# The last columns of the final product and their norm: two pieces over two pairs of row blocks become three pieces over four

## The chip, the cores and the metric

The kernel runs on one core of a Trainium2 chip. On that core five engines work side by side: TensorE (PE in the profile, PEld for its weight loads), VectorE (DVE), ScalarE (ACT), GpSimd (POOL) and SyncE (SP), which issues the DMA transfers. Each engine executes its own instructions strictly in the order in which the program gives them, and waits where an operand or a buffer is not ready. The metric is the device time of one execution in microseconds.

## The reference, cut to what matters

The reference is one layer of a hybrid decoder on 1024 positions of width 1024, and a norm at its end:

```
h = rmsnorm(x);  p = h @ W_in
x = x + concat(gated delta rule(p), gated linear recurrence(p)) @ W_out
x = x + relu(rmsnorm(x) @ W1)**2 @ W2          # W1: 1024 x 4096, W2: 4096 x 1024
y = x * rsqrt(mean(x*x, axis=-1) + 1e-6) * final_norm_w
```

The change touches the end of the last two lines: a part of the product with W2, the sum of squares over the 1024 channels, its reciprocal square root, and the multiplication of each value by that root and by the channel's weight in `final_norm_w`.

## The kernel before, in words

Data lie with channels on the 128 partitions and positions in the free dimension. A tile is 128 channels by 512 positions (a slab), and the 1024 channels of the result are eight such blocks, here called 0 to 7, for each of two halves of the positions. There are 84 slabs and eight PSUM banks, and both are handed on from use to use.

`layer()` does not issue instructions while it runs. It records each operation with a due time in a plan (class `Plan`, L181). At the end `Plan.emit` (L281) walks through time with its own cost model (`Plan.price`, L260, and for TensorE the cost handed to `pl.unit`), takes for each engine the operation that is ready with the smallest due time, and issues it at L371. So nearly every instruction of the profile stands at L371 and is told apart by the names of its tiles. The order that comes out is fixed in the program; if on the chip something takes longer than the model thinks, the engine waits and does not look for other work.

The product with W2 is done with seven block products in place of eight, in the scheme of Strassen and Winograd: the contraction is cut into 16 groups, the weights of each group into four blocks, and product *i* multiplies a sum of weight blocks v*i* with a sum of activation blocks u*i*. Four stages hold the products (1,7), (6,5), (2,4) and (3). Here only the last stage matters, product 3. For each group *g* DVE computes the block v3 as a difference (written over the loaded slab `w2r`, with the saved sum `s`), ACT rounds it to a high part `v3h` and DVE computes the low part `v3l`; in the same way u3 is loaded as `ur` and split into `u3h` and `u3l`. For each of four output blocks *d* and each group, `mm3` issues three matmuls into one PSUM bank `p`: u3h with v3h, u3l with v3h, u3h with v3l. All have a weight tile of 128 x 128 and a moving tile of up to 512 columns, which are positions.

In stage 3, groups 0 to 13 (NG - 2) run pair by pair over 512 columns into four banks. Behind group 13 DVE adds the four banks to the slabs `u2[d]` (in the profile `u<-p,u`), which hold the other products and the residual `x2` (`u<-x,u`). Then the last two groups, 14 and 15, run in two halves of 256 columns, four banks each, and for each half:

- DVE adds the bank to `u2[d]`, ACT squares the sum (`sq`), and ACT writes it once more multiplied by the norm weight (`xf`);
- `normed` (L1332) sums the squares over channels with matmuls whose weight is a tile of squares and whose moving tile is one column, `onesd` (`n3p`, one per 128 positions and tile of squares);
- ACT takes the square root, DVE the reciprocal and a Newton step (`ms`, `n3r`, `rst`), and a matmul spreads the result over the partitions (`n3b`);
- DVE multiplies `n3b` with each of the eight weighted blocks, four that ACT weighted earlier (`p5`, written over themselves; in the rows `p__9614` and the like) and four of `xf`, into slabs `ot` that hold two blocks of 256 columns each, and SP issues one DMA of 256 KB for each.

The due times of the products come first with half 0, then half 1; the additions and the squares have earlier due times than the products, so each engine takes them as soon as the cost model has them ready. The other three quarters of the result (blocks of positions or channels that are ready earlier) are normed in stage 3 beside the products.

Of the kernel before, what the change touches and what calls it, by code (L numbers as in the profile page):

```python
# [9 lines left out]
AF = mybir.ActivationFunctionType  # L10
ALU = mybir.AluOpType
# [19 lines left out]
DO = [0, 4, 1, 5, 2, 6, 3, 7]  # L31
KEEP_T = 8
LOOK = 4
SLACK = 1.0
LAND = 2.0
EPS = 1e-6
# [349 lines left out]
def layer(ctx: ExitStack, tc: tile.TileContext, xT, win, wba, prm, cst, wga, wgx, wout, w1, w2, out):  # L386
# [3 lines left out]
    pl = Plan()  # L390
    pe, ve, ac, gp, sy = (pl.engine(n) for n in engines)
# [9 lines left out]
    def slab(nm, dt=F32):  # L401
        return pl.tile(sp, [P, 512], dt, "s", nm)
# [4 lines left out]
    def bank(nm):  # L407
        return pl.tile(mpool, [P, 512], F32, "m", nm)
# [29 lines left out]
    PIECE = 0.68  # L438

    def mm3(ps, w, x, first, last, order=((0, 0), (0, 1), (1, 0))):  # L440
        n = 0
        for a, b in order:
            pe.matmul(ps, lhsT=w[a], rhs=x[b], start=first and n == 0, stop=last and n == 2)
            n += 1
# [9 lines left out]
    def par(nm, i=0, n=1):  # L454
        o = PRM[nm][0]
        return pr[:, o + i:o + i + n]
# [17 lines left out]
    with pl.at(due=-5000.0):  # L474
        wz = slab("wz")
        ve.memset(wz, 0.0)
        ps = bank("wz")
# [500 lines left out]
    def chain(t):  # L978
        return pl.at(due=t)
# [9 lines left out]
    with pl.at(due=-2000.0):  # L989
        for hf in range(2):  # L990
# [3 lines left out]
            for k in range(KT):  # L994
                pl.due = -2000.0 + 10 * k + 100 * hf
                if hf == 0:
                    xraw[0, k] = slab("xraw")
                    sy.dma_start(out=xraw[0, k], in_=xT[k * P:(k + 1) * P, hs])
                    if k in (0, 2, 4):
                        n = 4 if k == 4 else 2  # L1000
# [87 lines left out]
    for i in range(2, len(MT)):  # L1088
        mt = MT[i]
        split(i + 1)  # L1090
        for hf in range(2):
            ps = gemm(i if hf == 0 else None, f"pj{mt}", KT, lambda k: (ksl(wt[mt], k), (xh[hf][k], xl[hf][k])), 10000.0 + when(i))
# [41 lines left out]
    for n, d in enumerate(DO):  # L1134
        i = len(MT) + n
        t = when(i)
        split(i + 1)
        for hf in range(2):
            ps = gemm(i if hf == 0 else None, "po", KT, lambda k: (ksl(wt["o", d], EO[k]), M3[EO[k], hf]), 10000.0 + t)
# [5 lines left out]
            with chain(t + 7 + 7 * hf):  # L1145
# [3 lines left out]
                x = bm[d, hf] = slab("bm")  # L1149
# [17 lines left out]
    NG = NF // 2  # L1167
# [37 lines left out]
    for g in range(NG):  # L1205
        t = tf(g)
# [61 lines left out]
    def ts(st, g):  # L1268
        return begin[st] + g * 2.72 * len(STAGES[st])
# [50 lines left out]
    def wsl(g, i, d):  # L1320
        return tuple(t[:, d * P:(d + 1) * P] for t in W2[g, i])
# [9 lines left out]

    def normed(X, parts, a, n, t, lead, end):  # L1332

        m = n // P
        one = bank("n3p") if len(parts) == 1 else None
        pn = [one[:, c:c + 1] if one is not None else bank("n3p")[:, 0:1] for c in range(m)]
        for k, (x, ready) in enumerate(parts):
            with chain(ready):
                with pl.unit(0.12 * m):
                    for c in range(m):  # L1340
                        pe.matmul(pn[c], lhsT=x[:, c * P:(c + 1) * P], rhs=onesd, start=k == 0, stop=k == len(parts) - 1)
        with chain(t):
            r, v = small("n3r", [P, 4])[:, 0:m], small("ms", [P, 4])[:, 0:m]
            if end:
                for c in range(m):
                    ac.activation(out=r[:, c:c + 1], in_=pn[c], func=AF.Sqrt, bias=eps)
                    ve.tensor_scalar_add(out=v[:, c:c + 1], in0=pn[c], scalar1=EPS)
                ve.reciprocal(out=r, in_=r)
                newton(r, v)
            else:  # L1350
                ve.tensor_scalar_add(out=v, in0=one[:, 0:m], scalar1=EPS)
                rsqrt(r, v)
            pb = bank("n3b")
            with pl.unit(0.22 * m):
                rows(pb, r, m)
            g = 512 // n
            for j, d in enumerate(lead):
                if j % g == 0:
                    ot = slab("ot")
                y = ot[:, j % g * n:j % g * n + n]  # L1360
                if not end:
                    ve.scalar_tensor_tensor(out=y, in0=X[d], scalar=par("fnw", d), in1=pb[:, 0:n], op0=ALU.mult, op1=ALU.mult)
                else:
                    ve.tensor_tensor(out=y, in0=pb[:, 0:n], in1=X[d], op=ALU.mult)
                if (j + 1) % g == 0:
                    b = lead[j + 1 - g]
                    sy.dma_start(out=out[b * P:(b + g) * P, a:a + n].rearrange("(d p) t -> p d t", p=P),
                                 in_=ot.rearrange("p (d t) -> p d t", d=g))

    def squares(x, n=512):  # L1370
        y = slab("sq3")[:, 0:n]
        ac.activation(out=y, in_=x, func=AF.Square)
        return y
# [4 lines left out]
        residual[2] += [(x, (d + o, hf), 1 + 4 * n + d) for d in range(4)]  # L1378
    residual[3] = [(u2, (d, 1), 3 + 2 * d) for d in range(4)]
    for st, prods in enumerate(STAGES):  # L1380
        tail = 2 if st == 3 else 0
        pd = {}
        for g0 in range(0, NG, 2):
            gs = (g0, g0 + 1)
            for g in gs:
                get2(st, g)
            if st == 3 and g0 == NG - tail:
                break
            end = g0 == NG - tail - 2
            for d in range(4):  # L1390
                for i in prods:
                    if g0 == 0:
                        pd[i, d] = bank("p2")
                    for g in gs:
                        with pl.at(due=10000.0 + ts(st, g0) + 0.1 * d, keep={"m": 0}), pl.unit(PIECE):
                            mm3(pd[i, d], wsl(g, i, d), UU[g, i], g == 0, end and g == gs[1])
                        if d == 0 and i == prods[-1]:
                            seen[st * NG + g] = pl.ops[-1]
                    if not end:
                        continue  # L1400
                    ps = pd[i, d]
                    with chain(ts(st, g0) - 100):
                        if i in (1, 7, 5):
                            x = {1: p1, 7: u3, 5: p5}[i][d] = slab(f"p{i}_")
                            ac.copy(out=x, in_=ps)
                        elif i == 6:
                            u2[d] = slab("u2")
                            ve.tensor_tensor(out=u2[d], in0=ps, in1=p1[d], op=ALU.add)
                        elif i == 2:
                            plus(p1[d], ps)  # L1410
                        elif i == 4:
                            plus(u3[d], ps)
                        else:
                            plus(u2[d], ps)
            for x, k, g in residual[st]:
                if g in gs:
                    with chain(ts(st, g) + 3):
                        plus(x[k[0] % 4], load_x2(*k, st, g))
                        if x is p5:
                            y = squares(p5[k[0] % 4])  # L1420
                            if k[0] == 4:
                                ss = y
                            else:
                                plus(ss, y)
        t = begin[st] + 87
        if st == 1:

            with chain(t + 5):
                for d in range(4):
                    plus(u3[d], u2[d])  # L1430
                    plus(u2[d], p5[d])
                    plus(p5[d], u3[d])
        if st == 2:
            with chain(t - 40):
                s1 = None
                for x in [p1[d] for d in range(4)] + [u3[d] for d in range(4)]:
                    y = squares(x)
                    if s1 is None:
                        s1 = y
                    else:  # L1440
                        plus(s1, y)
            normed([p1[d] for d in range(4)] + [u3[d] for d in range(4)], [(s1, t - 40)], 0, 512, t - 30, list(range(KT)), False)

    t = ts(3, NG - 2)
    with pl.at(due=-1000.0, gate=seen[3 * NG + 4]):
        ac.activation(out=one("root", [P, 1]), in_=onesd, func=AF.Sqrt, bias=eps)
    with chain(t - 60):
        for d in range(4):
            ac.activation(out=p5[d], in_=p5[d], func=AF.Copy, scale=par("fnw", d + 4))
    for o in (0, 256):  # L1450
        qs = slice(o, o + 256)
        parts = []
        xs = {}
        for d in range(4):
            ps = bank("p2")[:, 0:256]
            for g in range(NG - 2, NG):
                with pl.at(due=10000.0 + t + o / 50 + 0.1 * d), pl.unit(PIECE / 2):
                    mm3(ps, wsl(g, 3, d), tuple(x[:, qs] for x in UU[g, 3]), g == NG - 2, g == NG - 1)
            with chain(t - 100):
                x = u2[d][:, qs]  # L1460
                plus(x, ps)
                parts.append((squares(x, 256), t))
                xs[d] = slab("xf")[:, 0:256]
                ac.activation(out=xs[d], in_=x, func=AF.Copy, scale=par("fnw", d))
        parts.insert(1, (ss[:, qs], t))
        X = [xs[d] for d in range(4)] + [p5[d][:, qs] for d in range(4)]
        normed(X, parts, 512 + o, 256, t + o / 50, [4, 5, 6, 7, 0, 1, 2, 3], True)

    pl.emit(engines, caps)

# [62 lines left out]
```

## Time and profile before

| what | value |
| --- | --- |
| three timed runs | 1111.16, 1112.57, 1112.77 us; median 1112.57 |
| the profiled execution | 1111.17 us, its span 1109.4 us |
| PE busy | 1089.9 us, 98% of the span |
| PEld busy | 898.4 us, 81% |
| DVE busy | 855.8 us, 77% |
| ACT busy | 559.0 us, 50% |
| POOL busy | 101.2 us, 9% |
| share of PE in the chain of work that ended last | 81% |
| DMA | mean 136 GB/s over the span |

The profile is that of one execution. Its durations and starts are in microseconds from the start of the span, and what the chip needs before and after the span is in the execution's own time. [...] Matmuls follow each other in a pipeline, so a row of one matmul is longer than the distance from its start to the next one's start; that distance is what a matmul costs when many stand in a row. A row "x4" is four instructions of one kind in succession. A matmul in full precision, as `n3p` and `n3b` are, appears as two passes, and so as twice as many rows as the program has instructions.

### The profile page before, as it was taken

The page shows a single profiled execution, that of the slowest core. Times are in us where ns is not written, and L with a number is a line of the kernel's source. Part 1 is how long each engine was busy: PE and PEld are TensorE (multiplying, and loading weights), DVE is VectorE, ACT ScalarE, POOL GpSimd, SP SyncE. Part 2 cuts the span into 40 slices and gives each one's busy share as a digit, 9 for nine tenths or more (in the row PEclk, how much of TensorE's full clock was granted, in tenths as well). Part 3 has the DMA queues.
Part 4 walks back from the last instruction along what each step waited for, and adds up shares of the span by engine and source line. Part 5 has one row for each costly group of instructions (what it writes and reads, how often), then busy time and mean ns, then how long its engine had stood idle before and what let it go on. Part 6 is the DMA issues. An engine that isn't in the chain of part 4 may idle for free.

```text
span 1109.4 us, 15927 instructions
## 1 busy us (share of the span) xinstructions
PE 1089.9 (98%) x5439; PEld 898.4 (81%) x5439; DVE 855.8 (77%) x1656; ACT 559.0 (50%) x1144; POOL 101.2 (9%) x282
## 2 busy tenths in 40 slices
PE   8999999999999999999999999999999999999996
PEld 6788877888887778888888888888888888888885
DVE  7868575696779777598988888887965767775786
ACT  8568545453485955453433333333544544464443
POOL 0002654736000000000000000000000000000000
PEclk9999999999999999999999999999999999999997
DMA  6122132031110144433634344434856565576382
GB/s 238 39 77 82 30 101 46 28 91 27 42 39 19 39 138 145 145 104 130 212 142 155 144 166 143 171 138 173 285 179 215 183 204 189 198 244 233 131 293 78
DMA packets 88128, 150.77 MB, mean 136 GB/s; under 512 B 22344, under 2 KB 25072, under 8 KB 88048
## 3 DMA queue, kind: packets, MB, share of 16 engines
q1 hardware_dynamic: 88048, 149.77, 40.2%
q8 instruction: 42, 0.69, 0.3%
q14 instruction: 38, 0.31, 0.1%
HBM read 110.91 MB, written 38.82 MB: 135 GB/s over the span
## 4 chain that ended last, share of the span: by engine, by line
PE 81%; DVE 5%; POOL 5%; ACT 3%; issue 2%; SPq 2%; DMA 1%; DVEq 0%; POOLq 0%; ACTq 0%
PE p L371 28%; PE pf L371 28%; PE pj L371 11%; PE po L371 7%; POOL V L371 2%; POOL tm L371 2%; SPq L371 2%; PE pvs L371 1%; DVE y L371 1%; PE psr L371 1%; PE psO L371 1%; DVE ig L371 1%; PE psba L371 1%; ACT rg L371 1%; PE psZ L371 1%
## 5 line engine op out<-in xcount | busy, mean ns | idle before, releaser
L371 PE MATMUL pj<-xh,w 128*128 128x512 f32 x704 | 246.6, 406 | 0.2 <-DVE U L371 0.2
L371 PEld LDWEIGHTS pj<-xh,w 128*128 128x128 f32 x704 | 132.7, 188 | 27.3 <-DVE U L371 0.4
L371 PE MATMUL pj<-xl,w 128*128 128x512 f32 x352 | 137.7, 391 | 0.0
L371 ACT ACTIVATE c<-c 128x512 f32<-128x512 f32 x64 | 40.4, 632 | 86.3 <-DVE c L371 80.8
L371 ACT CAST w<-r 128x512 fp32r<-128x512 f32 (+1 forms) x62 | 51.3, 829 | 60.6 <-PE pf L371 36.4
L371 PE MATMUL po<-mxh,w 128*128 128x512 f32 x256 | 78.9, 389 | 0.0
L371 PEld LDWEIGHTS pj<-xl,w 128*128 128x128 f32 x352 | 66.8, 190 | 10.1
L371 DVE SCALAR_TENSOR_TENSOR y<-p,pr,y 128x512 f32<-128x512 f32 (+3 forms) x96 | 71.3, 747 | 4.1 <-ACT y L371 3.1
L371 DVE TENSOR_TENSOR w<-r,w 128x512 fp32r<-128x512 f32 (+1 forms) x62 | 58.8, 949 | 18.3 <-ACT w L371 17.9
L371 POOL TENSOR_TENSOR tm<-V,N 128x60 f32<-128x60 f32 (+24 forms) x124 | 46.6, 376 | 133.1 <-DMA N<-bn 91.8
L371 PEld LDWEIGHTS po<-mxh,w 128*128 128x128 f32 x256 | 48.1, 188 | 9.9
L371 PE MATMUL po<-mxl,w 128*128 128x512 f32 x128 | 49.9, 390 | 1.5 <-DVE mxl L371 1.5
L371 POOL TENSOR_TENSOR V<-V,tm 128x60 f32<-128x60 f32 (+24 forms) x124 | 47.8, 385 | 9.7
L371 DVE SCALAR_TENSOR_TENSOR c<-c,n2B 128x512 f32<-128x512 f32 x64 | 43.7, 687 | 1.2
L371 PE MATMUL pf<-B6h,w 128*128 128x512 f32 x128 | 42.5, 391 | 0.0
L371 PE MATMUL pf<-B5h,w 128*128 128x512 f32 x128 | 42.5, 393 | 0.0
L371 ACT ACT_TABLE_LOAD x29 | 37.2, 1283 | 1.2 <-PEq L1526 0.7
L371 DVE TENSOR_TENSOR c<-pf,u 128x512 f32<-128x512 f32 x48 | 32.7, 684 | 0.5
L371 DVE TENSOR_TENSOR p<-pj,n1B 128x512 f32<-128x512 f32 x28 | 19.2, 686 | 17.5 <-PE pj L371 17.4
L371 ACT CAST v6h<-s 128x512 fp32r<-128x512 f32 x16 | 10.0, 623 | 40.2 <-DVE s L371 40.2
L371 PEld LDWEIGHTS po<-mxl,w 128*128 128x128 f32 x128 | 24.0, 188 | 6.9 <-DVE mxl L371 1.9
L371 PEld LDWEIGHTS pf<-B5h,w 128*128 128x128 f32 x128 | 24.0, 188 | 6.8 <-DVE c L371 1.9
(515 smaller groups left out, 2982.2 us busy)
## 6 DMA issues: line engine op xcount, KB each, us to landing
w2r<-w SPq DMA_DIRECT2D x112, 256.0 KB, 3.4
ur<-ud SPq DMA_DIRECT2D x112, 256.0 KB, 4.9
r<-w SPq DMA_DIRECT2D x32, 512.0 KB, 3.7
ud<-c SPq DMA_DIRECT2D x64, 256.0 KB, 2.1
ud<-ut SPq DMA_DIRECT2D x48, 256.0 KB, 2.2
r<-win SPq DMA_DIRECT2D x22, 512.0 KB, 3.7
xraw<-xT SPq DMA_DIRECT2D x16, 256.0 KB, 5.3
r<-wout SPq DMA_DIRECT2D x8, 512.0 KB, 4.2
```

The lines of the kernel that those rows point to most:

```text
L371: getattr(engines[e], method)(*[v.ap() if isinstance(v, View) else v for v in args], **{k: v.ap() if isinstance(v, View) else v for k, v i ...
```

## The change

The last four groups (12 to 15) are now held back in place of the last two, and run in three pieces of 256, 128 and 128 columns in place of two halves. The cost that the plan is told for three matmuls is now a formula in their width. The weighted copies `xf` and the earlier weighting of `p5` go; the last multiply takes the weight as a third operand (`scalar_tensor_tensor`) and gets a due time 20 us later than the rest of its piece. An `ot` slab holds at most two blocks, so that pieces of 128 columns leave in DMAs of 128 KB, whose rows are 128 values long. Everything before group 12 of stage 3 stands on PE and on SP as it stood. In the rows below, `p_...` with a number is a PSUM bank.

```diff
@@ -31,6 +31,7 @@
 DO = [0, 4, 1, 5, 2, 6, 3, 7]
 KEEP_T = 8
 LOOK = 4
+TAIL = 4
 SLACK = 1.0
 LAND = 2.0
 EPS = 1e-6
@@ -1353,19 +1354,17 @@
             pb = bank("n3b")
             with pl.unit(0.22 * m):
                 rows(pb, r, m)
-            g = 512 // n
+            g = min(512 // n, 2)
             for j, d in enumerate(lead):
                 if j % g == 0:
                     ot = slab("ot")
                 y = ot[:, j % g * n:j % g * n + n]
-                if not end:
+                with chain(t + 20):
                     ve.scalar_tensor_tensor(out=y, in0=X[d], scalar=par("fnw", d), in1=pb[:, 0:n], op0=ALU.mult, op1=ALU.mult)
-                else:
-                    ve.tensor_tensor(out=y, in0=pb[:, 0:n], in1=X[d], op=ALU.mult)
                 if (j + 1) % g == 0:
                     b = lead[j + 1 - g]
                     sy.dma_start(out=out[b * P:(b + g) * P, a:a + n].rearrange("(d p) t -> p d t", p=P),
-                                 in_=ot.rearrange("p (d t) -> p d t", d=g))
+                                 in_=ot[:, 0:g * n].rearrange("p (d t) -> p d t", d=g))
 
     def squares(x, n=512):
         y = slab("sq3")[:, 0:n]
@@ -1378,14 +1377,14 @@
         residual[2] += [(x, (d + o, hf), 1 + 4 * n + d) for d in range(4)]
     residual[3] = [(u2, (d, 1), 3 + 2 * d) for d in range(4)]
     for st, prods in enumerate(STAGES):
-        tail = 2 if st == 3 else 0
+        tail = TAIL if st == 3 else 0
         pd = {}
         for g0 in range(0, NG, 2):
             gs = (g0, g0 + 1)
             for g in gs:
                 get2(st, g)
-            if st == 3 and g0 == NG - tail:
-                break
+            if g0 >= NG - tail:
+                continue
             end = g0 == NG - tail - 2
             for d in range(4):
                 for i in prods:
@@ -1441,30 +1440,24 @@
                         plus(s1, y)
             normed([p1[d] for d in range(4)] + [u3[d] for d in range(4)], [(s1, t - 40)], 0, 512, t - 30, list(range(KT)), False)
 
-    t = ts(3, NG - 2)
+    t = ts(3, NG - TAIL)
     with pl.at(due=-1000.0, gate=seen[3 * NG + 4]):
         ac.activation(out=one("root", [P, 1]), in_=onesd, func=AF.Sqrt, bias=eps)
-    with chain(t - 60):
+    for o, n in ((0, 256), (256, 128), (384, 128)):
+        qs = slice(o, o + n)
+        parts = []
         for d in range(4):
-            ac.activation(out=p5[d], in_=p5[d], func=AF.Copy, scale=par("fnw", d + 4))
-    for o in (0, 256):
-        qs = slice(o, o + 256)
-        parts = []
-        xs = {}
-        for d in range(4):
-            ps = bank("p2")[:, 0:256]
-            for g in range(NG - 2, NG):
-                with pl.at(due=10000.0 + t + o / 50 + 0.1 * d), pl.unit(PIECE / 2):
-                    mm3(ps, wsl(g, 3, d), tuple(x[:, qs] for x in UU[g, 3]), g == NG - 2, g == NG - 1)
+            ps = bank("p2")[:, 0:n]
+            for g in range(NG - TAIL, NG):
+                with pl.at(due=10000.0 + t + o / 50 + 0.1 * d), pl.unit(3 * (n + 32) / 2400):
+                    mm3(ps, wsl(g, 3, d), tuple(x[:, qs] for x in UU[g, 3]), g == NG - TAIL, g == NG - 1)
             with chain(t - 100):
                 x = u2[d][:, qs]
                 plus(x, ps)
-                parts.append((squares(x, 256), t))
-                xs[d] = slab("xf")[:, 0:256]
-                ac.activation(out=xs[d], in_=x, func=AF.Copy, scale=par("fnw", d))
+                parts.append((squares(x, n), t))
         parts.insert(1, (ss[:, qs], t))
-        X = [xs[d] for d in range(4)] + [p5[d][:, qs] for d in range(4)]
-        normed(X, parts, 512 + o, 256, t + o / 50, [4, 5, 6, 7, 0, 1, 2, 3], True)
+        X = [u2[d][:, qs] for d in range(4)] + [p5[d][:, qs] for d in range(4)]
+        normed(X, parts, 512 + o, n, t + o / 50, [4, 5, 6, 7, 0, 1, 2, 3], True)
 
     pl.emit(engines, caps)
 
```

Three places show what the plan makes of it. The first is DVE at group 12 of stage 3, before; `s_8529` and `s_8562` are the saved sums of groups 12 and 13, and `v3l` and the first `u3l` behind it belong to group 12.

```order
L371 TENSOR_TENSOR w2r<-w2r,s_8529 128x512
L371 TENSOR_TENSOR u_9664<-x_10768,u_9664 128x512
L371 TENSOR_TENSOR v3l<-w2r,v3h 128x512
L371 TENSOR_TENSOR u3l<-ur,u3h 128x512
L371 TENSOR_TENSOR w2r<-w2r,s_8562 128x512
```

The same place now, where `p_10512`, `p_10527` and `p_10544` are the banks of the products up to group 11.

```order
L372 TENSOR_TENSOR w2r<-w2r,s_8529 128x512
L372 TENSOR_TENSOR u_9664<-x_10764,u_9664 128x512
L372 TENSOR_TENSOR u_9600<-p_10512,u_9600 128x512
L372 TENSOR_TENSOR u_9630<-p_10527,u_9630 128x512
L372 TENSOR_TENSOR v3l<-w2r,v3h 128x512
L372 TENSOR_TENSOR u_9664<-p_10544,u_9664 128x512
L372 TENSOR_TENSOR u3l<-ur,u3h 128x512
L372 TENSOR_TENSOR w2r<-w2r,s_8562 128x512
```

Three additions from PSUM have moved in among the preparations of group 12, two ahead of `v3l` and one more ahead of `u3l`.

The second place is the end of PE's order, before: the last product's last two matmuls, the sums of squares (`n3p`) of the second half and the broadcast of its result.

```order
L371 MATMUL p_10954<-u3l,v3h 128x256
L371 MATMUL p_10954<-u3h,v3l 128x256
L371 MATMUL n3p<-onesd,sq_11009 128x1 x2
L371 MATMUL n3p<-onesd,sq_11019 128x1 x2
L371 MATMUL n3p<-onesd,sq_9848 128x1 x2
L371 MATMUL n3p<-onesd,sq_11031 128x1 x2
L371 MATMUL n3p<-onesd,sq_11039 128x1 x2
L371 MATMUL n3p<-onesd,sq_11045 128x1 x2
L371 MATMUL n3b<-cs,n3r 128x128 x4
```

The end of PE's order now, in the last bank of the third piece.

```order
L372 MATMUL p_11126<-u3l,v3h 128x128
L372 MATMUL p_11126<-u3h,v3l 128x128
L372 MATMUL n3p<-onesd,sq_11124 128x1
L372 MATMUL n3b<-cs,n3r 128x128
L372 MATMUL p_11126<-u3h,v3h 128x128
L372 MATMUL p_11126<-u3l,v3h 128x128
L372 MATMUL p_11126<-u3h,v3l 128x128
L372 MATMUL p_11126<-u3h,v3h 128x128
L372 MATMUL p_11126<-u3l,v3h 128x128
L372 MATMUL p_11126<-u3h,v3l 128x128
L372 MATMUL n3p<-onesd,sq_11139 128x1
L372 MATMUL n3p<-onesd,sq_11156 128x1
```

The sums of squares now stand between the products, and two of them are left behind the last; the broadcast of the second piece stands ahead of the last six matmuls.

The third place is the end of DVE's order, before: from the sums of squares of both halves over the Newton step to the first multiply.

```order
L371 TENSOR_SCALAR ms<-n3p 128x1 x4
L371 RECIPROCAL n3r<-n3r 128x2
L371 TENSOR_TENSOR rst<-n3r 128x2
L371 RECIPROCAL n3r<-n3r 128x2
L371 SCALAR_TENSOR_TENSOR rst<-rst,ms 128x2
L371 TENSOR_TENSOR rst<-n3r 128x2
L371 SCALAR_TENSOR_TENSOR n3r<-rst,n3r 128x2
L371 SCALAR_TENSOR_TENSOR rst<-rst,ms 128x2
L371 SCALAR_TENSOR_TENSOR n3r<-rst,n3r 128x2
L371 TENSOR_TENSOR ot<-n3b,p__9614 128x256
```

The Newton step of the third piece now, and the first multiply that uses it.

```order
L372 TENSOR_SCALAR ms<-n3p 128x1
L372 SCALAR_TENSOR_TENSOR ot<-u_9600,pr,n3b 128x128
L372 RECIPROCAL n3r<-n3r 128x1
L372 SCALAR_TENSOR_TENSOR ot<-u_9630,pr,n3b 128x128
L372 TENSOR_TENSOR rst<-n3r 128x1
L372 SCALAR_TENSOR_TENSOR ot<-u_9664,pr,n3b 128x128
L372 SCALAR_TENSOR_TENSOR rst<-rst,ms 128x1
L372 SCALAR_TENSOR_TENSOR ot<-u_9688,pr,n3b 128x128
L372 SCALAR_TENSOR_TENSOR n3r<-rst,n3r 128x1
L372 SCALAR_TENSOR_TENSOR ot<-p__9614,pr,n3b 128x128
```

Four multiplies of the second piece stand between the small operations of the third, and eight of the third follow.

## Rows read from the trace of the kernel before

**Rows 1.** The chain that ended last: start us, us, what.

```profile
1061.33 30.14 PE p L371 x150
...
1098.88 1.21 PE n3b L371 x4
```

**Rows 2.** Busy time, granted clock and DMA share of three stretches.

```profile
core 0: us, PE busy (x) PEld busy (x) DVE busy (x) ACT busy (x) POOL busy (x), PEclk, DMA share, GB/s
1086.60:1094.40 7.80, 7.80 (x68) 7.78 (x67) 5.60 (x13) 4.10 (x11) 0.00 (x0) 1.00 0.00 1
1096.00:1098.00 2.00, 1.62 (x12) 1.36 (x11) 0.34 (x3) 2.00 (x7) 0.00 (x0) 0.95 0.00 0
1101.00:1109.40 8.40, 0.00 (x0) 0.00 (x0) 4.50 (x14) 0.00 (x0) 0.00 (x0) 0.50 0.75 250
```

**Rows 3.** PE's timeline around and behind group 12: start us, us, engine, line, operation, tiles.

```profile
1079.54 0.39 PE L371 MATMUL p<-u3h,v3l 128*128 128x512 f32 x1
...
1081.13 0.39 PE L371 MATMUL p<-u3h,v3h 128*128 128x512 f32 x1
...
1086.57 0.28 PE L371 MATMUL p<-u3h,v3h 128*128 128x256 f32 x1
1086.68 0.28 PE L371 MATMUL p<-u3l,v3h 128*128 128x256 f32 x1
...
1091.31 0.95 PE L371 MATMUL n3p<-onesd,sq 128*128 128x1 f32 x8
...
1092.56 0.50 PE L371 MATMUL n3p<-onesd,sq 128*128 128x1 f32 x4
...
1094.05 0.28 PE L371 MATMUL p<-u3h,v3l 128*128 128x256 f32 x1
```

**Rows 4.** The timeline of weight loads, around two matmuls of 32 columns and eight of one.

```profile
63.24 0.19 PEld L371 LDWEIGHTS psgc<-gl,utr 128*128 128x128 f32 x1
63.35 0.19 PEld L371 LDWEIGHTS pj<-xh,w 128*128 128x128 f32 x1
63.46 0.19 PEld L371 LDWEIGHTS pj<-xl,w 128*128 128x128 f32 x1
...
1091.19 0.98 PEld L371 LDWEIGHTS n3p<-onesd,sq 128*128 128x128 f32 x8
```

**Rows 5.** PE's timeline, the broadcast of an earlier quarter of the result.

```profile
1060.28 1.05 PE L371 MATMUL n3b<-cs,n3r 128*128 128x128 f32 x8
```

**Rows 6.** DVE's timeline: multiplies with the weight, additions from PSUM, multiplies at the end.

```profile
1061.82 0.74 DVE L371 SCALAR_TENSOR_TENSOR ot<-p__8776,pr,n3b 128x512 f32<-128x512 f32 x1
1062.48 0.74 DVE L371 SCALAR_TENSOR_TENSOR ot<-p__8808,pr,n3b 128x512 f32<-128x512 f32 x1
...
1085.09 2.48 DVE L371 TENSOR_TENSOR u<-p,u 128x512 f32<-128x512 f32 x4
...
1094.37 0.42 DVE L371 TENSOR_TENSOR u<-p,u 128x256 f32<-128x256 f32 x1 [0.38 <-PE p L371]
...
1101.45 1.41 DVE L371 TENSOR_TENSOR ot<-n3b,xf 128x256 f32<-128x256 f32 x4
```

**Rows 7.** DVE's timeline, the low part of u3 for group 12.

```profile
1080.00 0.68 DVE L371 TENSOR_TENSOR u3l<-ur,u3h 128x512 fp32r<-128x512 f32 x1
```

**Rows 8.** ACT groups from 1085 us (count | busy, mean ns | idle); DVE's Newton step.

```profile
L371 ACT ACTIVATE sq<-u 128x256 f32<-128x256 f32 x8 | 3.3, 411 | 2.5 <-DVE u L371 1.7 <-PE n3p L371 0.4 <-ACT xf L371 0.3
L371 ACT ACTIVATE n3r<-n3p,eps 128x1 f32<-128x1 f32 x4 | 0.8, 251 | 0.0
...
1098.31 0.17 DVE L371 RECIPROCAL n3r<-n3r 128x2 f32<-128x2 f32 x1
1098.39 0.14 DVE L371 SCALAR_TENSOR_TENSOR rst<-rst,ms 128x2 f32<-128x2 f32 x1
```

**Rows 9.** The output tile from 1099 us: its issues, and the time to landing.

```profile
L371 SPq DMA_DIRECT2D outT<-ot x8: 372/372/397, 1100.9 to 1105.5; - x8
...
DMA to landing us min/median/max: 2.2/2.6/2.9
```

## The prediction, made before the changed kernel ran

> **What bounds the kernel now.** I read the page first, then the chain that ended last, then the busy time and clock of three stretches at the end, then the timelines of TensorE (PE), VectorE (DVE), ScalarE (ACT) and the DMA queue there. The chain shows one run of PE products that lasts 30 us, up to the last pieces of stage 3 [rows 1]: until 1094.3 us the kernel goes as fast as PE issues matmuls. [...] So two regimes meet at 1094.3: before it, anything added to PE is paid in full; after it comes a serial tail of 1109.4 - 1094.3 = 15.1 us (squares, norm, 16 multiplies, DMA). The change shortens the tail and loads PE before it. The order of everything up to 1081.1 us is the same on PE and on the DMA queue, so I count from there.
>
> **The change part by part.** PE's timeline gives the spacing of matmuls: the part that differs starts at 1081.13 with 24 products of 512 columns and reaches the 256-wide ones at 1086.57, 0.227 us each; the 256-wide ones come 0.12 us apart (1086.57, 1086.68), and the last one ends at 1094.05 + 0.28 = 1094.33 [rows 3].
>
> *Products.* Gone: 4 banks x 2 groups x 3 = 24 matmuls of 512, 24 x 0.227 = 5.4 us. The 256-wide ones stay 48 in number (before 2 halves x 4 banks x 2 groups x 3, now 1 piece x 4 x 4 x 3). New: 2 pieces x 4 x 4 x 3 = 96 matmuls of 128 columns. No product of 128 columns in this number format stands in the trace, so its spacing is bounded. Below by streaming: 128 columns at the slope between 256 and 512 columns ((0.227 - 0.120)/256 per column) give 0.120 - 0.054 = 0.066 us, which is also what the kernel's own cost term 3(n+32)/2400 assumes. Above by the 256-wide row, 0.120. Which end is near is told by what each matmul brings with it: a weight load of 128 columns, as many loads as matmuls. Where the moving side is nearly empty the loads alone set the pace: around the two 32-column products of the same format the loads start at 63.24, 63.35 and 63.46, 0.11 us apart, and eight loads for products of one column take 0.98 us, (0.98 - 0.19)/7 = 0.113 [rows 4]. A 128-column product streams for less than that, so I take 0.112: 96 x 0.112 = 10.75 us. Half the columns cost as much as the whole. Net of the products: 10.75 - 5.4 = +5.3 us.
>
> [...]
>
> *Norm work between the products.* Sums of squares (n3p) and row broadcasts (n3b) are full-precision matmuls of two passes each, 0.112 us a pass [rows 4]; n3b costs the same at full clock, eight passes in 1.05 us, (1.05 - 0.28)/7 = 0.11 [rows 5]. Before, 16 passes of n3p stood ahead of the last product (eight, then four behind each of two banks [rows 3]); the order now puts 20 (first piece) + 10 (second) + 6 (third) of n3p and 4 + 2 of n3b there: 42. Net 26 x 0.112 = +2.9 us.
>
> *A new wait at the start.* DVE now has three additions u<-p between the preparation of group 12 (v3l, u3l) and what preceded it. The one of bank 1 waits for a product that starts at 1079.54 and takes 0.39 [rows 3]; with a hop of 0.04 (the last product ends at 1094.33, its addition starts at 1094.37 [rows 6]) it starts at 1079.97. Behind it stand v3l, the addition of bank 2 and u3l, 0.60 us apart (four additions in 2.48 us [rows 6]; 0.62 with waits): u3l starts at 1081.82 and ends at 1082.50. Before, it ran at 1080.00 [rows 7]. PE's second matmul of group 12 reads it and could go at 1081.25; it goes at 1082.57. Cost: +1.3 us. Behind u3l on DVE queue the preparations of groups 13 to 15, nine operations at 0.60 to about 1088.6; PE asks for group 15 at 1089.2, so no second stall follows, with 0.6 us to spare.
>
> *End of the products:* 1094.33 + 5.3 + 2.9 + 1.3 = 1103.8.
>
> *The tail.* From the last product: addition of 128 columns 0.30 (256 take 0.42 [rows 6], less 128 at the slope of 1.06 ns a column below); square 0.30 (256: 0.41), one norm product of two passes 0.11 + 0.25 = 0.36, square root 0.25 [rows 8]; reciprocal and Newton step. Into that step DVE's order now mixes four multiplies of the second piece: five small operations, 0.08 apart [rows 8], the last 0.15 long, so 0.47, and four multiplies. A 256-wide multiply takes 0.33 (four in 1.41 us); with the weight as a third operand a 512-wide one takes 0.66 against 0.60, so +0.06 [rows 6]; 128 columns by the slope from 256 to 512 ((0.60 - 0.33)/256, 1.06 ns a column): 0.33 - 0.14 + 0.06 = 0.25. Step: 0.47 + 4 x 0.25 = 1.5. Broadcast at full clock 0.39. Eight multiplies 8 x 0.25 + 0.08 = 2.1. Eight hops 0.4. DMA: a 256 KB output lands 2.2 us after its issue where the queue is empty, 2.9 at the end of before, where eight follow each other [rows 9]. At 250 GB/s over a DMA share of 0.75 [rows 2], 333 GB/s where busy, 256 KB move in 0.79 us, so 128 KB land in 2.2 - 0.4 = 1.8 if bytes decide. The new rows are 512 bytes long, as many per transfer as before; if their number decides, 2.2 plus a queue of 3 x 0.29, 3.1. No transfer of that kind stands in these rows; I take 1.87, since most of the 2.2 is no moving of bytes. To the span's end 0.95, as now. Sum 0.30 + 0.30 + 0.36 + 0.25 + 1.5 + 0.39 + 2.1 + 0.4 + 1.87 + 0.95 = 8.4 us against 15.1: -6.7 us. In it are what the edit wins: half the multiplies behind the last norm, no weighted copies (xf) on ACT, a broadcast at full clock (at the end of before four passes took 1.21 us, the clock being 0.50 [rows 1]). If the clock has fallen again by then, +0.25: in before it fell 3.5 us after the last product, here the broadcast comes 3.0 us after it.
>
> The four ACT multiplies of p5 by the weight, earlier in the stage, free ACT, which waits there anyway: nothing. Two multiplies on DVE now write buffers whose earlier output DMA must have landed; by the same spacings those DMAs are issued near 1098.4 and 1100.2 and land 2.2 us later, while the multiplies come after 1105.9: no cost, and several us of cover.
>
> **Sum:** +5.3 + 2.9 + 1.3 - 6.7 = +2.8 us: 1109.4 becomes 1112.2 in the span. The profiled execution took 1111.17 for its span of 1109.4; the three timed runs gave 1111.16, 1112.57 and 1112.77, so the profiled one is among the quick ones. Added to the median 1112.57 it is 1115.4, to the profiled run 1114.0; I say 1115.0.
>
> **Rivals.**
> - *128 columns stream at 0.066.* The loads hide behind the neighbours' streaming, as they do at 256 columns. Then PE gets 96 x 0.046 = 4.4 us back; DVE, whose order is fixed, would then give some back (its multiplies of piece one meet the additions of piece two), about 0.7. Time: 2.8 - 3.7 = -0.9, 1111.3. It decides from a spacing under 0.08, where the sum passes zero. Against it: the 0.11 us rows of loads with an almost empty moving side. Not slower, hence the other side.
> [...]
> - *No stall at group 12.* If the additions of banks 1 and 2 come early enough, +1.5, 1113.7. Against it: PE's bank order in the rows fixes when bank 1 ends.
> - *Output DMAs of 512-byte rows cost as much as those of 1024.* The tail grows by up to 1.2: +4.0, 1116.2; with the clock fallen, 1116.4.
>
> **How the numbers follow.** Of the measurements here 0.2% (2.2 us) can be told from no change. Chances: the forecast 0.70, with +/-0.9 for summed estimates and the spread of runs, of which 0.14 falls under 2.2 us; stream-bound 0.08; in between 0.07; no stall 0.08; dearer DMA or clock 0.07. Slower by over 0.2%: 0.56 + 0.07 + 0.01 = 0.64. Faster by over 0.2%: 0.03, out of the stream-bound case, with the stall gone too (-2.2). Same: the rest, 0.33. The range for 8 in 10: from 1111.6 (stream-bound's upper half) to 1117.0 (dearer DMA and a slow run).
>
> **What would show it.** Right: products of 128 columns 0.11 us apart; a gap of about 1.3 us on PE near 1081.3 that ends with DVE's u3l; the last product ending near 1103.8; some 8.4 us from there to the end, with eight multiplies at 0.25 in it; DMAs landing within 2 us. Wrong: a spacing of 0.07 (then it is even or slightly faster), or no gap near 1081. Should PE stop again before group 15, or DVE's additions lag behind the products late in the stage, the result is worse than 1117.

## The result, and the profile after

The changed kernel takes 1121.65 us (median of 6 runs, 1120.40 to 1123.10) where the kernel before takes 1112.32 (6 runs): ratio 1.0085, 95% interval 1.0073 to 1.0096. It is 9.3 us slower; 2.8 were forecast (2.4 in the time given, 1115.0, against the median of then), and the measured time lies outside the range of 1111.6 to 1117.0. The direction and most terms held; one thing that no term contained cost 8.0 us: TensorE's granted clock fell from 1.00 to 0.50 while PE was busy throughout.

First the windows of the changed kernel, from its first piece to the end (columns as in [rows 2]; PEclk, the granted clock of TensorE as a share of its full speed, is the third figure from the right).

```profile
1081.20:1089.24 8.04, 8.04 (x71) 8.04 (x70) 7.42 (x15) 3.58 (x7) 0.00 (x0) 1.00 0.00 1
1089.24:1093.80 4.56, 4.56 (x43) 4.56 (x43) 1.55 (x8) 1.73 (x7) 0.00 (x0) 1.00 0.01 4
1093.90:1109.50 15.60, 15.60 (x75) 15.60 (x75) 5.26 (x19) 1.76 (x6) 0.00 (x0) 0.50 0.15 50
1110.00:1118.60 8.60, 1.38 (x4) 1.00 (x4) 4.64 (x21) 0.48 (x2) 0.00 (x0) 0.50 0.47 136
```

PE and its weight loads are busy 15.60 of 15.60 us in the third row, and the granted clock there is 0.50; in [rows 2] the products ran at 1.00 to their end. The clock fell at 1093.9 and did not return. PE's timeline shows what it was doing and what that did to the spacing.

```profile
1079.29 0.39 PE L372 MATMUL p<-u3h,v3l 128*128 128x512 f32 x1
1080.39 0.35 PE L372 MATMUL p<-u3h,v3h 128*128 128x256 f32 x1 [0.72 <-DVE u L372]
1080.90 0.38 PE L372 MATMUL p<-u3l,v3h 128*128 128x256 f32 x1 [0.15 <-DVE u3l L372]
1081.12 0.28 PE L372 MATMUL p<-u3h,v3l 128*128 128x256 f32 x1
...
1082.59 0.27 PE L372 MATMUL p<-u3h,v3h 128*128 128x128 f32 x1
1082.70 0.27 PE L372 MATMUL p<-u3l,v3h 128*128 128x128 f32 x1
...
1089.24 1.89 PE L372 MATMUL n3p<-onesd,sq 128*128 128x1 f32 x16
...
1091.37 1.00 PE L372 MATMUL n3p<-onesd,sq 128*128 128x1 f32 x8
...
1094.20 0.41 PE L372 MATMUL p<-u3h,v3l 128*128 128x128 f32 x1
1094.41 0.41 PE L372 MATMUL p<-u3h,v3h 128*128 128x128 f32 x1
...
1109.13 0.41 PE L372 MATMUL p<-u3h,v3l 128*128 128x128 f32 x1
```

Products of 128 columns come 0.11 us apart up to 1093.8 (1082.59, 1082.70) and 0.21 behind (1094.20, 1094.41). Ahead of the fall stand two bursts of one-column sums, 16 and 8 passes, with three narrow products between them; the second ends 1.6 us before the fall. The last product ends near 1109.56; DVE's addition begins behind it. The new stop near 1080 is there too. The end of the chain and the output DMAs answer to [rows 1, 9]:

```profile
1108.37 1.19 PE p L372 x6
1109.56 0.03 issue
1109.59 0.30 DVE u L372
...
1112.70 0.81 PE n3b L372 x2
1113.51 0.03 issue
1113.53 1.12 DVE ot L372 x4
```

```profile
L372 SPq DMA_DIRECT2D outT<-ot x12: 372/372/407, 1098.4 to 1115.7; - x12
...
DMA to landing us min/median/max: 1.8/1.9/2.2
```

The last product is now followed by 9.0 us (1118.6 - 1109.56) in place of 15.1.

The two profiles do not start even. Ahead of the change PE's order is the same in both, but the kernel before had a short fall of the clock early on (first row; second row, the changed kernel). Its products lie 0.31 us later near 187 us, ahead of that fall, and 1.64 us later at the start of stage 3 (1046.41 against 1044.77).

```profile
189.50:193.50 4.00, 4.00 (x41) 3.26 (x40) 3.14 (x16) 0.00 (x0) 0.00 (x0) 0.57 0.73 200
```

```profile
189.50:193.50 4.00, 3.68 (x48) 2.80 (x46) 3.51 (x17) 0.47 (x2) 0.00 (x0) 1.00 0.84 236
```

The profiled executions took 1120.43 and 1111.17 us. Counted from the start of stage 3, the changed kernel therefore loses 9.26 + 1.64 = 10.9 us in the profiles; the medians, in which such early falls come and go in both, say 9.3.

### The profile page after: what moved, and what is told of

The parts are those of the page before. It is cut to its first block, busy times and chain, and to the rows that moved or that the text cites. A ratio compares the mean times of both kernels' runs of the same rounds, so it can differ in the third digit from the quotient of the medians.

```text
span 1118.6 us, 16084 instructions
## 1 busy us (share of the span) xinstructions
PE 1100.8 (98%) x5511; PEld 910.5 (81%) x5511; DVE 859.0 (77%) x1672; ACT 553.6 (49%) x1136; POOL 100.6 (9%) x282
## 5 line engine op out<-in xcount | busy, mean ns | idle before, releaser
L372 PE MATMUL p<-u3h,v3h 128*128 128x512 f32 (+2 forms) x96 | 35.1, 366 | 0.7 <-DVE u L372 0.7
L372 PE MATMUL p<-u3l,v3h 128*128 128x512 f32 (+2 forms) x96 | 34.8, 362 | 0.2 <-DVE u3l L372 0.2
L372 PE MATMUL p<-u3h,v3l 128*128 128x512 f32 (+2 forms) x96 | 34.8, 363 | 0.0
```

The lines of the kernel that those rows point to most:

```text
L372: getattr(engines[e], method)(*[v.ap() if isinstance(v, View) else v for v in args], **{k: v.ap() if isinstance(v, View) else v for k, v i ...
```

## The experiments

The question was what let the clock fall: the narrow products (theory N), the bursts of one-column sums (theory S), PE's stop near 1080 (theory P), or more than one of them. Ratios are to the kernel before, run on the same chip each time (its median was 1109.36, 1110.23 and 1109.68 in the three sessions). Differences in us are the ratio's, times that median. The table gives the granted clock from the profile of each run; "passes" are those of one-column sums and of broadcasts among the products, group by group in their order.

| run | second and third piece | passes among them | clock | ratio, interval |
| --- | --- | --- | --- | --- |
| the change | 128 columns | **16**, 8, 2, 4, 2, ... | falls at 1093.9, stays down | 1.0085 (1.0073 to 1.0096) |
| e1 | 256 columns, half unused | **16**, 8, 2, 4, 2, ... | falls at 1090.2, back at 1097.1 | 1.0035 (1.0017 to 1.0054) |
| e2 | one piece of 256 | **20**, 8, 4, 4, 4 | falls at 1092.2, back at 1099.1 | 1.0009 (0.9996 to 1.0021) |
| e8 | 128 columns | **8**, 4, 4, 2 | falls at 1092.9, stays down | 1.0057 (1.0036 to 1.0077) |
| e5 | 128 columns | **4**, 2, 4, 2 | holds to the last product | 0.9989 (0.9979 to 0.9999) |
| e13 | 128 columns | **4**, 2 | holds to the last product | 1.0009 (0.9995 to 1.0023) |
| e12 | 128 columns | none | holds to the last product | 1.0071 (1.0046 to 1.0096) |

Each clock in the table is that of one profiled execution. Of the others the mean granted clock over the span is known. It is 0.985 to 0.989 in all six executions of the change (its profile, with the fall, has 0.989) and 0.996 to 0.998 in all ten of e5 (its profile, with a fall only behind the last product, has 0.996), so these two do not hang on one profile. In e13 it is 0.993 to 0.997 in twelve; the profiled one has 0.994, by estimate some 13 us at half clock (2 x 0.006 x its span of 1111.0), none of them between 1090.2 and 1099.2, where it is 1.00.

### e1: the same order, wide products

```diff
-            ps = bank("p2")[:, 0:n]
+            pw = bank("p2")[:, 0:256]
+            ws = slice(o // 256 * 256, o // 256 * 256 + 256)
+            ps = pw[:, o % 256:o % 256 + n]
-                    mm3(ps, ..., tuple(x[:, qs] for x in UU[g, 3]), ...)
+                    mm3(pw, ..., tuple(x[:, ws] for x in UU[g, 3]), ...)
```

> The changed kernel with the same order of instructions on every engine, but the 96 products of the second and third piece run over all 256 columns 256 to 511 (only the piece's own 128 are used). Theory N: narrow products (array half empty while weights load) are what let the TensorE clock fall at 1093.8 us. Then the clock stays at 1.00 up to the last product; 96 x (0.120 - 0.112) = +0.8 us, 76 instructions no longer at half clock -7.3, tail at full clock -0.7: 1121.65 + 0.8 - 7.3 - 0.7 = 1114.5 us. Theory S: the bursts of one-column sums of squares let it fall. Then it falls as before near 1094 and the time is about 1122.5. Theory P: PE's stop near 1080 let it fall: about 1122.5 too.

Measured: 1114.44 us, ratio 1.0035, 3.9 us above before, between the 2.2 of theory N and the 10.2 of S and P. The windows say why neither had it.

```profile
1079.10:1087.84 8.74, 8.74 (x74) 8.74 (x74) 7.93 (x15) 3.82 (x8) 0.00 (x0) 1.00 0.00 1
1087.84:1090.20 2.36, 2.36 (x24) 2.36 (x23) 0.51 (x3) 0.81 (x3) 0.00 (x0) 1.00 0.00 0
1090.30:1097.00 6.70, 6.70 (x33) 6.70 (x33) 1.35 (x9) 1.34 (x5) 0.00 (x0) 0.50 0.01 2
1097.10:1104.20 7.10, 7.10 (x63) 7.10 (x61) 4.69 (x16) 1.19 (x4) 0.00 (x0) 1.00 0.25 85
```

The clock falls at the bursts again, at the start of the second, with no narrow product in the kernel; so the bursts let it fall, against N. But after 6.8 us it is back, which in the changed kernel it never was in the 15.7 us up to the end of the last product; so the narrow products keep it down, against S alone. Only the width of the products differs between the two.

Two of the eight executions of e1 differ: 1111.32 and 1111.67 us, with a mean clock of 0.997 against 0.993 to 0.995 in the other six. A mean of 0.997 leaves some 6.7 us at half clock (2 x 0.003 x the span, an estimate), and the stretch at the end takes 5.7 us by itself in the profile:

```profile
1107.30:1113.00 5.70, 0.55 (x2) 0.26 (x2) 2.15 (x8) 0.00 (x0) 0.00 (x0) 0.50 0.48 138
```

So in these two the clock seems to have held through the same bursts, and they lie 2.1 us above before, near the 2.2 of N. Bursts among wide products let the clock fall in most executions of e1 and not in all. No profile of such an execution was taken, so the reason is open.

### e5: narrow products, few sums

```diff
-        normed(X, parts, 512 + o, n, t + o / 50, ...)
+        normed(X, parts[-1:], 512 + o, n, t + o / 50, ...)
```

> The changed kernel with only one of the five tiles of squares summed in each piece (four fifths of the sum of squares are left out); the 96 narrow products stay. 32 one-column passes fewer between the products: -3.6 us at 0.112. Theory N (narrow products): the clock falls all the same during the second or third piece, PEclk 0.50 at the last product, about 1118 us. Theory S (bursts of one-column passes): the clock stays at 1.00 up to the last product, a further -7.3 - 0.7: about 1110.3 us. Theory P (the stop near 1080): falls, 1118.

The kernel leaves out four of the five tiles of squares in each piece, so its result is not the layer's; it serves for the clock alone.

Measured: 1108.80 us, ratio 0.9989, 1.2 us below before; S said 2.0 below, N 5.7 above.

```profile
1089.00:1097.20 8.20, 8.20 (x74) 8.11 (x73) 4.54 (x20) 2.27 (x9) 0.00 (x0) 1.00 0.10 34
```

The narrow products run at full clock to the last one. The stop near 1080 is in this kernel too (its chain that ended last starts behind it at 1079.31, as the chain of the change does at 1080.85), so theory P falls.

### e2 and e4: the change without narrow products

```diff
-    for o, n in ((0, 256), (256, 128), (384, 128)):
+    for o, n in ((0, 256), (256, 256)):
```

and for e4 also

```diff
-TAIL = 4
+TAIL = 2
```

> The changed kernel with pieces of 256 and 256 columns over the four last groups, no product of 128. Against the kernel before: 96 x 0.120 for 24 x 0.227 + 48 x 0.120 = +0.3; 24 more one-column and broadcast passes between the products +2.7; stop at group 12 +1.3; tail shorter by 5.6 (eight multiplies of 0.39 after the last broadcast in place of sixteen and no weighted copies). Theory N: the clock stays at 1.00 up to the last product: -1.3, about 1111 us. Theory S: the burst of 20 + 8 passes ahead of the last 27 products lets the clock fall, some +3.5: about 1114.5.

> The kernel before with its two groups and two halves of 256 columns, and of the change only the norm weight in the last multiply and its due time 20 us later (no weighted copies). 12 more passes between the products +1.3; tail: no weighted copies on ACT, 16 multiplies at 0.39 in place of 0.33, but the first eight begin about 1 us after the last product: some 11.3 us in place of 15.1. -2.5: about 1109.8 us. If the multiplies of the first half hold up the second half's norm on DVE, nothing is won: 1112. The clock holds up to the last product by either theory.

e2 measured 1.0 us above before, between the -1.3 of N and the +2.2 of S. Its windows repeat e1: a burst of 20 and 8 passes, the fall, and the return while products of 256 columns run.

```profile
1090.10:1092.20 2.10, 2.10 (x22) 2.10 (x21) 0.67 (x2) 1.18 (x4) 0.00 (x0) 1.00 0.00 0
1092.30:1099.00 6.70, 6.70 (x33) 6.70 (x33) 2.60 (x10) 0.94 (x3) 0.00 (x0) 0.50 0.01 2
1099.10:1101.40 2.30, 2.30 (x21) 2.16 (x19) 1.88 (x5) 0.42 (x1) 0.00 (x0) 1.00 0.53 181
```

e4 measured 1108.92 us, ratio 0.9997 (0.9983 to 1.0011): no change, where 2.5 us were expected, and "the clock holds" was wrong. Its plan moved the first half's sums up, 20 passes ahead of the last nine products and 8 ahead of the last six; the clock fell at 1092.4, and the last products and 20 more passes ran at half of it:

```profile
1089.40:1092.40 3.00, 3.00 (x30) 3.00 (x29) 1.15 (x6) 1.46 (x5) 0.00 (x0) 1.00 0.00 0
1092.50:1097.80 5.30, 5.30 (x25) 5.20 (x25) 2.23 (x9) 1.51 (x4) 0.00 (x0) 0.50 0.00 0
```

So the weight in the last pass by itself wins nothing that can be measured here. That what it saves in the tail goes back through the clock is an estimate: 6 products and 16 passes at 0.1 us more each make 2.2 us, against the 2.5 expected.

### e6: the stop at group 12 set apart

```diff
-                    with chain(ts(st, g0) - 100):
+                    with chain(ts(st, g0) - 100 if st < 3 else ts(3, NG - 3) - 16):
```

> The changed kernel, with the due time of the additions from PSUM behind group 11 set back so that DVE prepares v3l and u3l of group 12 ahead of the second and third addition. Theory: PE's stop of 1.26 us near 1080 goes and nothing else changes; the clock falls all the same in the burst of one-column sums and stays down. That is the change's +9.3 us against before less 1.3: +8.0 us (ratio 1.0072). Rival: PE then waits for a free PSUM bank in place of u3l, and nothing is won: +9.3 us (1.0084). Rival: the stop was part of what let the clock fall: under +4 us.

Measured: 1121.60 us, ratio 1.0104 (1.0086 to 1.0122); no gain. The stop did not go, it moved:

```profile
1083.06 0.28 PE L372 MATMUL p<-u3l,v3h 128*128 128x256 f32 x1
1083.93 0.39 PE L372 MATMUL p<-u3h,v3l 128*128 128x256 f32 x1 [0.59 <-DVE v3l L372]
```

PE now waits for v3l of group 13: it starts 0.87 us behind its predecessor in place of 0.12, a stop of 0.75 where it was 1.3. The half us saved is not seen: counted from the start of stage 3, the clock fell 46.9 us in, against 49.1 in the changed kernel, and more narrow products ran at half clock. The rival named a wait in place of the wait, and that was right, though not for a bank. Whether the stop has a part in the fall, the third rival, this run does not test; e5 and e13 have the stop (in e13 a product at 1081.68, 1.10 us behind the one at 1080.58) and keep the clock.

### e8: the sums added on DVE

```diff
-                parts.append((squares(x, n), t))
-        parts.insert(1, (ss[:, qs], t))
+                y = squares(x, n)
+                if d < 3:
+                    plus(ss[:, qs], y)
+        parts = [(ss[:, qs], t), (y, t)]
```

> The changed kernel, but DVE adds the squares of the first three tiles of a piece to those of the older four, so that two tiles in place of five go through one-column matmuls; nothing is left out. Theory B (a burst of one-column matmuls lets the clock fall, narrow products then keep it down, but do not let it fall by themselves): some 26 passes fewer -2.9, clock 1.00 up to the last product -7.3, tail -0.7, one more addition on DVE's path +0.3: the change's +9.3 becomes -1.3 us against before (ratio 0.9988). Rival N2 (narrow products let it fall by themselves, only later): it falls within the last third of the narrow products, about +2 us (1.0018).

Measured: 1117.14 us, ratio 1.0057; both theories are missed, B by 7.6 us. The clock fell 2.1 us behind the start of a burst of only 8 passes, and stayed down:

```profile
1086.00:1090.90 4.90, 4.90 (x46) 4.90 (x45) 3.51 (x14) 2.43 (x7) 0.00 (x0) 1.00 0.00 0
1090.90:1092.80 1.90, 1.90 (x19) 1.90 (x19) 0.78 (x5) 0.79 (x3) 0.00 (x0) 1.00 0.04 9
1093.00:1102.50 9.50, 9.50 (x47) 9.50 (x46) 3.86 (x18) 1.19 (x4) 0.00 (x0) 0.50 0.08 28
```

This speaks against two separate causes: among wide products 8 passes let nothing fall in the profiles of the kernel before ([rows 2, 3]) and of e10 below, among narrow ones they did. These kernels differ in more than the width, so that it is the width that decides at 8 passes is argued and not shown. That left open whether narrow products alone would do it, only later.

### e12 and e13: narrow products with no sums, and with six passes

e12 sets the due time of all sums behind the products:

```diff
-                parts.append((squares(x, n), t))
-        parts.insert(1, (ss[:, qs], t))
+                parts.append((squares(x, n), 20000.0))
+        parts.insert(1, (ss[:, qs], 20000.0))
```

e13 adds all four squares on DVE:

```diff
-                parts.append((squares(x, n), t))
-        parts.insert(1, (ss[:, qs], t))
+                plus(ss[:, qs], squares(x, n))
+        parts = [(ss[:, qs], t)]
```

> The changed kernel with the due time of all sums of squares set behind the products: 75 products of 128 columns stand in a row and no one-column matmul or broadcast ahead of the last. Theory B2 (narrow products leave the clock near its edge, but only one-column passes among them tip it): granted clock 1.00 up to the last product and for a while behind it. Theory N2 (narrow products tip it by themselves, later): it falls within the 8.4 us of the 75 products. The time goes by the long tail (40 sums, 24 multiplies behind the last product, about +9 us): some +6 us against before by B2 (1.0054), +9 or more by N2.

> The changed kernel with all squares of a piece added up on DVE, so that one tile goes through the one-column matmuls (6 passes among the narrow products, behind the first 39 of them); nothing is left out. Theory B2: the clock holds up to the last product, as in the run few_sums, and the time is that run's -0.6 us against before plus 0.6 for four additions on DVE: about 0 (ratio 1.000). Theory N2: the clock falls among the last 36 narrow products as in the run dve_sums: +4 us (1.0036) or more.

e12 measured 1118.06 us, ratio 1.0071: +7.9 us, between the +6 of one theory and the +9 of the other, so the time says little. Its clock decides:

```profile
1089.30:1097.60 8.30, 8.30 (x77) 8.30 (x76) 2.59 (x9) 3.05 (x11) 0.00 (x0) 1.00 0.01 2
1097.60:1099.50 1.90, 1.90 (x19) 1.90 (x19) 0.29 (x1) 0.31 (x1) 0.00 (x0) 1.00 0.00 0
1099.60:1104.30 4.70, 4.70 (x24) 4.70 (x23) 1.14 (x9) 0.78 (x3) 0.00 (x0) 0.50 0.00 0
```

75 narrow products in a row, 8.3 us, hold the full clock; 1.9 us into the 40 one-column passes behind them it falls. e13 measured 1111.22 us, ratio 1.0009: the clock is 1.00 from 1090.2 to 1099.2, where the last 75 of its narrow products run; the 21 ahead of them come 0.11 us apart too. It is the changed kernel with the squares added elsewhere, and its ratio is 0.0076 below that of the change.

### e3: two groups in place of four

```diff
-TAIL = 4
+TAIL = 2
```

> The changed kernel with two groups held back in place of four, the pieces of 256, 128 and 128 kept. Against before: 48 x 0.112 for 24 x 0.120 +2.5; 28 passes more among the products +3.1; tail -6. Theory B: the burst of 16 + 8 one-column passes lets the clock fall near 1092 and the narrow products keep it down: +5.5 for some 36 products and 18 passes. About +5 us (1.0045). If the clock came back among the narrow products: +2 (1.0018).

Measured: 1115.47 us, ratio 1.0048 (1.0031 to 1.0066), 5.3 us as expected. The clock falls at 1092.9, behind 16 and 8 passes, and stays at 0.50 through the narrow products:

```profile
1088.60:1092.80 4.20, 4.20 (x40) 4.20 (x40) 1.66 (x8) 2.05 (x8) 0.00 (x0) 1.00 0.00 0
1093.00:1101.30 8.30, 8.30 (x39) 8.13 (x39) 3.04 (x14) 1.39 (x5) 0.00 (x0) 0.50 0.10 34
```

### e9 and e10: versions that keep the clock

Both are the changed kernel with pieces of 256 and 256 columns (the edit of e2) and the squares added on DVE (the edit of e8); e9 has two groups (the edit of e3), e10 four and the later additions (the edit of e6).

> Two groups and two halves of 256 as before, norm weight in the last multiply, and the squares added on DVE as in the run named dve_sums. No one-column pass is left ahead of the last product: -1.8; tail: 16 passes, 16 multiplies of 0.39 begin some 2.5 us after the last product: 11.9 in place of 15.1, -3.2. In all -3.5 to -5 us against before (ratio 0.996). If the multiplies alone bound the tail as in the run named weight_last, -1.5 (0.9987). The clock stays at 1.00 up to the last product by theory B.

> Four groups, two pieces of 256, weight in the last multiply, squares added on DVE, and the additions behind group 11 set back as in the run named no_stall. Products +0.3, passes ahead of the last product as many as before, no stop at group 12, tail some 10 us in place of 15.1: -4.7 us against before (ratio 0.9958). By theory B the clock stays at 1.00 up to the last product; if it falls within the second piece all the same, -1.5 (0.9987).

e9 measured 1106.47 us, ratio 0.9965 (0.9954 to 0.9976); e10 1106.17, ratio 0.9959 (0.9946 to 0.9973). Both beat both kernels, by the amount expected. In e10 the clock is 1.00 to the last product, with 8 passes among its last products:

```profile
1085.50:1095.40 9.90, 9.88 (x81) 9.67 (x81) 9.37 (x26) 4.38 (x11) 0.00 (x0) 1.00 0.00 1
```

## Why the prediction was wrong

**What failed.** The step is the price of what stands on PE: "96 x 0.112" for the products and "26 x 0.112" for the passes. Both durations were right at a granted clock of 1.00, and at 0.50 neither held. From 1093.82, where the product that ran into the fall starts, to 1109.35, where the pass behind the last product starts, PE began 57 products and 16 passes in 15.53 us; at 0.112 these 73 take 8.18. That is +7.35. In the tail, two passes of n3p at half clock took 0.60 where 0.36 stood for them, and the broadcast 0.81 where 0.39 stood: +0.66. Together this is 8.0 of the 10.9 us lost in the profiles, and what is left, 2.9, is the forecast sum of 2.8 to 0.1.

The prediction reckoned with a fall of the clock only behind the last product, and gave it 0.25 us and a part of a 0.07 chance. The trace of before had the counter-evidence, in a stretch that I passed over as the start of the tail. Behind its last product PE went on working:

```profile
1094.40:1097.80 3.40, 2.95 (x23) 2.64 (x22) 0.68 (x4) 2.97 (x10) 0.00 (x0) 1.00 0.00 0
```

It was busy 2.95 of 3.40 us with one-column sums, and at the end of that stretch, at 1097.8, the clock fell. Moving such sums in among products that are themselves only half as wide as the stream that had held the clock was the thing to price; the sum moved 26 passes there and asked only for their time.

No idle time of PE stands at the fall: from 1081.20 up to 1093.80 PE was busy all 12.60 us (8.04 and 4.56 in the windows of the changed kernel), at 1.00, and behind it 15.60 of 15.60, at 0.50. Here the clock was lost, and stayed lost, without any gap.

**What held.** Narrow products at full clock are 0.11 us apart, as their weight loads are (1082.53, 1082.64 and 1082.75 on PEld), and not the 0.066 estimated for streaming; only the first one behind a wide product is followed after 0.07 (1082.30, 1082.37). So the rival *stream-bound* is out. The chances also give 0.07 to a spacing in between (0.066 and 0.112); no run shows such a spacing, in its place stand the 0.11 us of the change and of e5, e12 and e13. The 42 passes in front of the last product are there. So is the stop at group 12: the first product comes 1.10 us behind its predecessor in place of 0.227, by the profile's releaser behind one of DVE's additions, and the second 0.51 in place of 0.12, behind u3l: 1.26 in all against 1.3, though I had it at the second product alone. No second stop came. (Nine operations at 0.60 behind u3l end at 1087.9 and not at 1088.6 as the prediction has it; a tenth, an addition `u<-x`, stands among them in the trace, and with it 1088.6 is about right.) The tail without the clock is 9.0 - 0.7 = 8.3 us against 8.4: multiplies of 128 columns 0.26 apart (0.25), the eight output DMAs of 128 KB landing in 1.8 us in the median (1.87); the rival of dear 512-byte rows is out. The direction was right for a smaller reason than the true one.

**What the change would be worth.** From e13 to the change, 1.0009 to 1.0085, is what the clock and 36 passes ahead of the last product cost, less the additions that e13 makes on DVE. Even without them nothing is won over the kernel before: narrow products cost nearly what wide ones do (0.112 us for 128 columns, 0.120 for 256), and that takes back the shorter tail, as the prediction had it. The versions that win keep the wide products: e10 is 0.0050 below e13, 5.5 us, and 96 x 0.112 - 48 x 0.120 = 5.0 us would be the products' part of that, an estimate from their spacings (e10 also sets additions back).

## What to carry to other kernels

A busy PE was no proof of its clock here (0.50 with PE busy 15.60 of 15.60 us): price every PE instruction at both levels (a product of 128 columns took 0.112 us at 1.00 and 0.213 at 0.50), and look in the trace of before at what the array was doing when the clock last fell, not only at whether it was idle. Group one-column matmuls behind the wide products, or add their inputs up on an engine with time to spare, before they are moved in among products; the harm was largest where the products around them were narrow (1.0085 in the change, 1.0035 in e1), and these did not bring the clock back in any run here (15.7 us in the change, 9.5 in e8, 8.3 in e3). Cutting matmuls of 256 columns to 128 saved next to nothing per matmul here: 256 columns cost 0.120 us and 128 cost 0.112, the spacing of their weight loads.

## What the runs showed of the hardware that was not expected

- Granted clock 0.50 with PE and weight loads busy 100% for 15.6 us (the change), and again for 9.5 us in e8.
- Products of 128 columns held a clock that was up (8.3 us in e12) but did not bring it back in 15.7 us (the change) or 9.5 (e8); stretches with products of 256 columns brought it back after 6.8 us in e1 and e2.
- In the change a product of 128 columns took 0.213 us at 0.50 and 0.112 at 1.00.
- Why the clock falls at one moment and not at another these runs do not tell. e6 lost it 2.2 us earlier in the stage than the change, with the same bursts, and two of the eight executions of e1 leave no room for a fall among the products.
